# Regrouping the small matmuls of one hybrid encoder step: decode values in fours, state reads behind the scores, state updates over four banks

## The chip, the cores and the metric

The kernel runs on one core of one Trainium2 chip. The metric is the device time of one execution in microseconds (us), median of several. The kernel before took 2405.88 us (three runs, 2405.13 to 2412.4).

TensorE (PE) multiplies a stationary operand (at most 128 rows by 128 columns) with a moving one of up to 512 columns and writes into PSUM, which has eight banks of 512 fp32 values per partition. VectorE (DVE), ScalarE (ACT) and GpSimd (POOL) do the elementwise work. SyncE (SP), ACT and POOL issue DMA transfers; each of these queues works strictly in order, so a transfer that waits holds up whatever stands behind it.

## The reference

One step of a layer with two groups of eight heads, on a prompt of 1024 frames and on 8 running streams of 16 frames each (the "sample", 128 rows):

```python
h = rms_norm(x, norm_pre)
q_sb, k_sb, v_sb, gate_sb, q_r, k_r, v_r, gate_r = project(h, w_in, pos)   # 2048 x 8192
# stick-breaking heads; the sample has 1024 cached keys and values per stream
z = q @ k.T * d ** -0.5
a = where(strict, exp(log_sigmoid(z) + later(log_sigmoid(-z))), 0)
o_sb = a @ v
# retention heads, chunkwise; the sample starts from a state of 128 x 128 per stream and head
o_r   = (q_r k_r' * decay) @ v_r + decay_read * (q_r @ S)
S_new = gamma ** n * S + (k_r * decay_write)' @ v_r
y = concat(head_norm(o_sb) * silu(gate_sb), head_norm(o_r) * silu(gate_r)) @ w_out
x = x + rms_norm(y, norm_post)
```

For the sample this means, per head: scores against 8 x 1024 cached keys, a weighted sum over 8 x 1024 cached values, a read of eight 128 x 128 states, and an update of those eight states.

## The kernel before

**Groups and projections.** The rows are worked on in two groups: the first has four prompt tiles of 128 rows and the sample tile (640 rows), the second the other four prompt tiles. For every head of a group the kernel projects queries, keys, values and gates of both branches. Operands are split into a high and a low part, and each product is three matmuls (lines 227 and 286). These products fill PE; everything else is fitted between them. The accumulators `acc0` and `acc1` with two buffers each take four of the eight PSUM banks. The other four are two score banks (`psz`, tile `z`, used in turn by `score_tile`), one bank `psa` (tile `pa`, given by `acc_tile`) and one bank `psd` (tile `pd`, the decode sums).

**The hand-written clock.** Side work is written as Python generators, each wrapped in a `Job`. `tick()` is called once behind each of the product's three operand pairs at line 227, and once behind each group of three matmuls at line 286; it adds one to the clock and runs the first job that is due up to its next `yield`, whose number says after how many steps it wants to go on. A step is thus one pair of product matmuls in the first group. `drain(job)` calls `tick()` again and again without any product until a job has ended. It is called where the next head takes over a buffer: `ret_queries` drains the retention job behind its projection (line 910), `attention` drains the stick-breaking and the decode jobs (lines 934 and 949). Behind this stands the framework's own planner: it puts each engine's instructions in an order by what it takes to be ready, earlier program text first, so that an instruction may slip behind products that follow it in the text. `tied` and `issue_after` pin an instruction behind another one of its engine.

**The decode job** (lines 623 to 743), one per head, first group only. It loads the cached keys in 16 pieces of 128 x 512 from POOL's queue, transposes each on DVE, and after pieces 8 and 16 runs one score set at line 659: 16 instructions (8 fp32 matmuls, each two instructions) with 32 stationary columns, four streams side by side in the array's column strips. The pieces are `D_ZC` = 12 steps apart. Then come sigmoids, a product scan, a trip through DRAM that transposes the weights by blocks (`turn_out`, `turn_in`), and the value sum. The values are 8 tiles `vc` of 512 KB each, held in `V_BUFS` = 6 buffers and loaded by SP (line 687). The sum (lines 717 to 731) first multiplies the sample's own 128 rows (line 718) and then takes the 8 tiles two at a time: a pause of 18 steps, one set of 16 instructions with 32 stationary columns (line 726), and the loads of the next tiles into the buffers set free (tiles 6 and 7, behind the first set). Right behind the last set DVE copies the sum out of `pd` (lines 733 and 735).

**The retention job** (lines 745 to 857), one per head and group. For the sample it loads the states in four tiles `st` (two streams each), waits 18 steps, multiplies the sample's own part (line 810) and reads the states with 8 instructions of 32 columns (line 813), all into one `pa` bank. 9 steps later ACT and DVE take the result out, and the update follows in two halves, 9 steps apart: each takes the two score banks, multiplies with a contraction of 32 rows only (line 830, 8 instructions, two pairs of streams side by side in the array's row strips), lets DVE add to the states (line 833) and stores them. Then the output is normalised, turned through DRAM (32 + 32 steps) and gated; in doing so it writes the tiles `rk` and `rg`, which the next head uses again.

Of the kernel before, what the change touches and what calls it, by code (L numbers as in the profile page):

```python
# [9 lines left out]
F32 = mybir.dt.float32  # L10
F32R = mybir.dt.float32r
AF = mybir.ActivationFunctionType
ALU = mybir.AluOpType
# [3 lines left out]
P = 128  # L17
# [4 lines left out]
DS = 16  # L22
# [10 lines left out]
KC_AHEAD = 2  # L33
D_DEC = 2
D_NAT = (8, 11)
D_TR = (3, 7)
D_ZP = (2, 2)
D_Z0 = (19, 11)
D_AV = (9, 11)
# [2 lines left out]
D_KN = 40  # L42
D_VC = 9
V_BUFS = 6
D_RET = (9, 5)
D_TO = (32, 23)
D_TA = (14, 0)
# [7 lines left out]
LOG_GAMMA = [math.log(1.0 - 2.0 ** (-5.0 - h)) for h in range(H)]  # L55
# [3 lines left out]
def tile_hybrid_step(  # L59
# [26 lines left out]
    nc = tc.nc  # L86
# [61 lines left out]
    phase = [0]  # L148
# [151 lines left out]
    with ExitStack() as s1:  # L300
# [47 lines left out]
        with tc.tile_pool(name="p0", bufs=2) as p0, tc.tile_pool(name="p0s", bufs=1) as p0s, tc.tile_pool(  # L348
            name="p0p", bufs=4, space=PSUM
# [100 lines left out]
        psa = s1.enter_context(tc.tile_pool(name="psa", bufs=1, space=PSUM))  # L450
        psd = late.enter_context(tc.tile_pool(name="psd", bufs=1, space=PSUM))
# [108 lines left out]
        def stick_breaking(g, h, out, q2, k2, rest):  # L560
# [3 lines left out]
            for step in range(len(todo) + lag):  # L564
# [55 lines left out]
                    out.done(i)  # L620
                yield D_AV[phase[0]]

        def decode(h, qs, rest):
            i = 4
            out = Out(1, "do")
# [4 lines left out]
            n = PAST + P  # L630
# [21 lines left out]
            for m in range(-KC_AHEAD, 2 * NB + 1):  # L652
                if m > 0 and m % NB == 0:
                    s, _, _ = chunk(m - NB)
                    z = score_tile("zc")
                    for j in range(2):
                        for c in range(4):
                            r = slice(32 * c, 32 * c + 32)
                            mm = nc.tensor.matmul(  # L659
                                z[r, :],  # L660
                                qp[:, j, r],
                                ready[2 * j + c // 2][:, c % 2, :],
                                start=(j == 0),
                                stop=(j == 1),
                            )
                            if j == c == 0:

                                tc.add_manual_dep(
                                    mm.ins,
                                    turned.ins.name,  # L670
                                    mybir.DependencyInfo(
                                        mybir.DependencyClass.NoSync, mybir.DependencyReason.SCHED_ONLY
                                    ),
                                    reason="a set at a time",
                                )
                    ready = []
                    sigmoids(kp, be, s * 512, z)
                if 0 <= m < 2 * NB:
                    if m % 2 == 0:
                        ready.append(ip.tile([P, 2, 512], F32, name="kcT", tag="kv", bufs=V_BUFS))  # L680
                    turned = nc.vector.transpose(ready[-1][:, m % 2, :], loaded.pop(0))  # L681
                    yield D_ZC
                if m + KC_AHEAD < 2 * NB:
                    loaded.append(load(m + KC_AHEAD))
            def load_v(k):
                vc = ip.tile([P, NB, P], F32, name="vc", tag="kv", bufs=V_BUFS)
                ld = nc.sync.dma_start(
                    vc, cache_v[0, :, k * P : (k + 1) * P, h, :].rearrange("b p d -> p b d")
                )
                if 2 <= k < V_BUFS:  # L690
                    tied(ld)
                return vc
# [24 lines left out]
            po = psd.tile([P, 512], F32, name="pd", tag="pd")  # L717
            nc.tensor.matmul(po[:, 2 * P : 3 * P], at[:, 8, :], vn[:, i, :], start=True, stop=True)

            for k0 in range(0, 8, 2):  # L720
                yield 2 * D_VC
                for k in (k0, k0 + 1):
                    vc = values.pop(0)
                    for c in range(4):
                        r = slice(32 * c, 32 * c + 32)
                        nc.tensor.matmul(  # L726
                            po[r, : 2 * P], at[:, k, r], vc[:, 2 * c : 2 * c + 2, :], start=(k == 0), stop=(k == 7)
                        )
                for k in (k0, k0 + 1):
                    if k + V_BUFS < 8:  # L730
                        values.append(load_v(k + V_BUFS))
            od = out.o[:, 0, :]
            nc.vector.tensor_copy(od, po[:, 2 * P : 3 * P])
            for j in range(2):
# [65 lines left out]
        def sample_retention(h, out, sc, rq, rkn, rv):  # L800
            i = 4

            sts = []
            for c in range(4):
                st = ip.tile([P, 2, P], F32, name="st", tag="st", bufs=4)
                tied(nc.sync.dma_start(st, state_ret[0, 2 * c : 2 * c + 2, h].rearrange("b d e -> d b e")))
                sts.append(st)
            yield 2 * D_RET[phase[0]]
            po = acc_tile()
            nc.tensor.matmul(po[:, 2 * P : 3 * P], sc, rv[:, i, :], start=True, stop=True)  # L810
            for c in range(4):
                r = slice(32 * c, 32 * c + 32)
                nc.tensor.matmul(
                    po[r, : 2 * P], rq[:, i * P + 32 * c : i * P + 32 * c + 32], sts[c], start=True, stop=True
                )
            yield D_RET[phase[0]]
            od = out.o[:, i, :]
            nc.scalar.activation(od, po[:, 2 * P : 3 * P], AF.Copy)
            for j in range(2):
                nc.vector.scalar_tensor_tensor(  # L820
                    od, po[:, j * P : (j + 1) * P], dec[:, h, 2 + j : 3 + j], od, ALU.mult, ALU.add
                )
            out.done(i)

            for c0 in (0, 2):
                pS = [score_tile(f"pSs{c}", (P, 2, P)) for c in range(2)]
                for j in range(2):
                    for c in range(2):
                        r = slice(32 * (c0 + c), 32 * (c0 + c) + 32)
                        nc.tensor.matmul(pS[c][:, j, :], rkn[r, i + j, :], rv[r, i, :], start=True, stop=True)  # L830
                for c in range(2):
                    st, b = sts[c0 + c], 2 * (c0 + c)
                    nc.vector.scalar_tensor_tensor(
                        st, st, math.exp(LOG_GAMMA[h] * DS), pS[c], ALU.mult, ALU.add
                    )
                    nc.scalar.dma_start(s_sample[0, b : b + 2, h].rearrange("b d e -> d b e"), st)
                yield D_RET[phase[0]]

        def ret_branch(gi, g, h, rq, rk, rv, rest):
            nt = len(g["tiles"])  # L840
# [367 lines left out]
```

## Time and profile before

| | |
|---|---|
| median of three runs | 2405.88 us |
| span of the profiled execution | 2398.4 us |
| mean granted TensorE clock in it | 0.994 |
| PE busy | 2331.4 us, 97% |
| DVE, ACT, POOL busy | 52%, 38%, 27% |
| first group's heads (about 130 to 1235 us) | PE busy 1078.65 of 1105 us |

The profiled execution is 7.5 us shorter than the median of the runs. A row of the timeline reads: start, duration, engine, line, operation, output<-inputs, rows*columns of the stationary operand, the moving operand, count of instructions, and in brackets the idle time before it with what ended that. Durations of matmuls include their way through the array and overlap; what a matmul costs is read from one start to the next. A row of the waits reads: who waited for whom, us in total, times, longest.

### The profile page before, as it was taken

What the parts mean: (1) busy time and instruction counts of PE and PEld (TensorE: products, weight loads), DVE (VectorE), ACT (ScalarE), POOL (GpSimd) and SP (SyncE); (2) the same over time, 40 slices, a digit from 0 to 9 for tenths busy, and PEclk for the clock granted to TensorE, in tenths of its full rate; (3) what the DMA queues carried; (4) which work ended last, traced back from release to release, by engine and by line L of the source; (5) the groups of instructions that cost most, each with busy time, mean ns of one, the idle gap of its engine ahead of it and who ended that gap; (6) DMA issues with size and microseconds to landing.
All of it is one profiled execution on the core that took longest, in us unless ns stands there. A gap on an engine that the chain in (4) does not pass through costs nothing.

```text
span 2398.4 us, 40493 instructions
## 1 busy us (share of the span) xinstructions
PE 2331.4 (97%) x14832; PEld 2093.7 (87%) x14832; DVE 1257.5 (52%) x2434; ACT 919.6 (38%) x1933; POOL 643.0 (27%) x1029
## 2 busy tenths in 40 slices
PE   7999999999999999998999999999999999999998
PEld 7998899999999999988878889889898887878787
DVE  7245545445554555445545554554554665564544
ACT  6323333333333333324433434343343454543343
POOL 3144353444344353443202112020221230000000
PEclk9999999999999999999999999999999999999999
DMA  7658879797889879798975565565565666765554
GB/s 244 164 131 209 162 169 196 169 203 166 184 179 194 184 167 194 176 198 198 200 191 151 139 157 149 133 157 146 142 160 139 157 177 181 231 207 176 191 182 132
DMA packets 674890, 418.68 MB, mean 175 GB/s; under 512 B 224513, under 2 KB 619777, under 8 KB 672257
## 3 DMA queue, kind: packets, MB, share of 16 engines
q1 hardware_dynamic: 524272, 285.99, 47.8%
q0 software_dynamic: 32256, 71.36, 13.6%
q10 hardware_dynamic: 118160, 58.74, 9.1%
q8 instruction: 116, 1.90, 0.4%
q14 instruction: 86, 0.70, 0.1%
HBM read 336.24 MB, written 79.69 MB: 173 GB/s over the span
## 4 chain that ended last, share of the span: by engine, by line
PE 87%; DVE 4%; DMA 4%; issue 2%; ACT 1%; POOL 1%; ACTq 0%; DVEq 0%; SPq 0%; POOLq 0%
PE acc L227 45%; PE accn L286 17%; PE a L1029 5%; PE a L1030 5%; PE a L1028 5%; PE pa L616 3%; PE z L586 2%; DMA wr<-w_in 1%; PE zc L659 1%; PE pd L726 1%; DMA mr<-s_h 1%; DVE wl L130 1%; PE pa L770 1%; DVE out L1090 1%; PE rs L752 1%
## 5 line engine op out<-in xcount | busy, mean ns | idle before, releaser
L227 PE MATMUL acc<-mh,wh 128*128 128x256 f32 (+2 forms) x2304 | 664.3, 341 | 6.4 <-ACT wh L129 6.0
L227 PE MATMUL acc<-ml,wh 128*128 128x384 f32 (+2 forms) x2304 | 663.0, 340 | 0.0
L130 DVE TENSOR_TENSOR wl<-wr,wh 128x512 fp32r<-128x512 f32 (+1 forms) x576 | 392.7, 688 | 515.5 <-ACT wh L129 508.3
L227 PE MATMUL acc<-mh,wl 128*128 128x256 f32 (+2 forms) x2304 | 658.9, 339 | 0.6 <-DVE wl L130 0.5
L129 ACT ACTIVATE wh<-wr 128x512 fp32r<-128x512 f32 (+1 forms) x576 | 356.9, 624 | 713.1 <-PE acc L227 243.4
L227 PEld LDWEIGHTS acc<-mh,wh 128*128 128x128 f32 x2304 | 420.2, 189 | 43.3 <-ACT wh L129 7.1
L227 PEld LDWEIGHTS acc<-mh,wl 128*128 128x128 f32 x2304 | 424.4, 189 | 31.4 <-issue 2.1
L227 PEld LDWEIGHTS acc<-ml,wh 128*128 128x128 f32 x2304 | 422.6, 189 | 33.2 <-issue 5.3
L643 POOL DMA_DIRECT2D kc<-cache_sb_k x512 | 332.4, 655 | 369.8 <-DVE kcT L681 207.5
L286 PE MATMUL accn<-whn,mh 128*128 128x256 f32 x1152 | 329.0, 287 | 0.9 <-ACT whn L129 0.8
L286 PE MATMUL accn<-wln,mh 128*128 128x256 f32 x1152 | 326.2, 283 | 0.7 <-DVE wln L130 0.7
L286 PE MATMUL accn<-whn,ml 128*128 128x256 f32 x1152 | 326.0, 283 | 0.0
L286 PEld LDWEIGHTS accn<-whn,mh 128*128 128x128 f32 x1152 | 220.5, 192 | 10.8 <-issue 6.7
L1029 PE MATMUL a<-wl,mh 128*128 128x512 f32 (+1 forms) x576 | 219.7, 381 | 7.8 <-DVE wl L130 7.8
L286 PEld LDWEIGHTS accn<-wln,mh 128*128 128x128 f32 x1152 | 221.2, 192 | 1.7 <-DVE wln L130 0.9
L286 PEld LDWEIGHTS accn<-whn,ml 128*128 128x128 f32 x1152 | 221.2, 192 | 0.0
L1030 PE MATMUL a<-wh,ml 128*128 128x512 f32 (+1 forms) x576 | 218.9, 380 | 0.0
L1028 PE MATMUL a<-wh,mh 128*128 128x512 f32 (+1 forms) x576 | 218.0, 380 | 0.0
L130 DVE TENSOR_TENSOR wln<-wrn,whn 128x512 fp32r<-128x512 f32 x128 | 87.5, 687 | 119.2 <-ACT whn L129 118.5
L129 ACT ACTIVATE whn<-wrn 128x512 fp32r<-128x512 f32 x128 | 80.1, 633 | 152.2 <-PE accn L286 69.8
L1029 PEld LDWEIGHTS a<-wl,mh 128*128 128x128 f32 x576 | 108.3, 188 | 30.5 <-DVE wl L130 9.9
L479 POOL DMA_DIRECT2D be<-s_be x128 | 94.2, 742 | 132.7 <-DMA s_be<-be 114.7
(189 smaller groups left out, 2604.8 us busy)
## 6 DMA issues: line engine op xcount, KB each, us to landing
wr<-w_in SPq DMA_DIRECT2D x384, 256.0 KB, 4.2
wr<-w_out SPq DMA_DIRECT2D x184, 256.0 KB, 3.6
wrn<-w_in SPq DMA_DIRECT2D x128, 256.0 KB, 3.1
kc<-cache_sb_k POOLq DMA_DIRECT2D x512, 64.0 KB, 4.5
vc<-cache_sb_v SPq DMA_DIRECT2D x64, 512.0 KB, 8.6
xt<-x_prompt SPq DMA_DIRECT2D x8, 1024.0 KB, 5.6
xr<-x_prompt SPq DMA_DIRECT2D x8, 1024.0 KB, 6.2
out<-out ACTq DMA_DIRECT2D x12, 512.0 KB, 2.9
```

Source lines behind the costliest of these rows:

```text
L129: nc.scalar.activation(hi, src, AF.Copy)
L130: nc.vector.tensor_tensor(lo, src, hi.bitcast(F32), ALU.subtract)
L227: last = nc.tensor.matmul(a[:, :m], lhs[:, j, :], rhs[w][:, j, o : o + m], start=(w == 0 and j == 0 and n == 0), stop=(w == KT // WQ - 1 a ...
L286: anchor[0] = nc.tensor.matmul(a, lhs[q][:, jj, ts], rhs[:, j, :], start=(w == 0 and j == 0 and n == 0 and t % 2 == 0), stop=(w == KT // 2 ...
L479: q.dma_start(raw[32 * i : 32 * i + 32, :].rearrange("p (k a) -> p k a", a=32), s[:, :, 32 * i : 32 * i + 32].rearrange("k (j b) a -> b (k ...
L586: nc.tensor.matmul(z[:, :c], q2[a][:, i * P : (i + 1) * P], k2[b][:, s : s + c], start=(m == 0), stop=(m == 2),)
L616: nc.tensor.matmul(po[:, :P], at[:, j, :], vn[:, j, :], start=(j == 0), stop=(j == t))
L643: nc.gpsimd.dma_start(kc[32 * i : 32 * i + 32, :].rearrange("p (k d) -> p k d", d=32), cache_k[0, 2 * c + j, s * 512 : (s + 1) * 512, h, 3 ...
L659: mm = nc.tensor.matmul(z[r, :], qp[:, j, r], ready[2 * j + c // 2][:, c % 2, :], start=(j == 0), stop=(j == 1),)
L1028: nc.tensor.matmul(a[:, :width], hi[q][:, j, ts], wh, start=(k == 0), stop=False)
L1029: nc.tensor.matmul(a[:, :width], hi[q][:, j, ts], wl, start=False, stop=False)
L1030: nc.tensor.matmul(a[:, :width], lo[q][:, j, ts], wh, start=False, stop=(k == KT - 1))
```

## The change

Five things change, all in code that runs in the first group (the constants for the second group stay as they are):

- The value sum takes four key tiles at a time: two sets of 32 instructions, each after a pause of 36 steps, instead of four sets of 16 after 18. The loads of tiles 6 and 7 stand behind the first set of four.
- The copies out of `pd` come 6 steps after the last set (`D_SUM`), not at once.
- The state reads are put on a list. The decode job of whichever head is then running calls the list right behind the matmuls of its next score set, and pins the reads behind the last of them. The retention job looks every 2 steps whether that has happened, up to 70 times, and issues the reads itself if not. The sample's own part (line 810) moves behind the reads. The results are taken out 3 steps later (`D_OFF`) instead of 9.
- The state update is one set of 16 instructions over four banks (both score banks, `pa` and `pd`), with the first instruction of the older score bank in front and the rest pinned behind the first two; 3 steps later come DVE's four additions and the four stores.
- The pause in front of the transposed weights' use, `D_TR`, goes from 3 to 7 steps in the first group; it stands in the decode job in front of line 718 and in the stick-breaking job in front of its last value product.

```diff
-D_TR = (3, 7)
+D_TR = (7, 7)
...
+V_SET = 4
+D_SUM = 6
+N_READ = 70
+D_OFF = 3
...
+        waiting = []
+
+        def with_scores():
+            while waiting:
+                waiting.pop(0)()
...
                     ready = []
+                    with tc.issue_after(mm.ins):
+                        with_scores()
                     sigmoids(kp, be, s * 512, z)
...
-            for k0 in range(0, 8, 2):
-                yield 2 * D_VC
-                for k in (k0, k0 + 1):
+            for k0 in range(0, 8, V_SET):
+                yield V_SET * D_VC
+                for k in range(k0, k0 + V_SET):
                     vc = values.pop(0)
...
+            yield D_SUM
             od = out.o[:, 0, :]
...
             yield 2 * D_RET[phase[0]]
-            po = acc_tile()
-            nc.tensor.matmul(po[:, 2 * P : 3 * P], sc, rv[:, i, :], start=True, stop=True)
-            for c in range(4):
-                r = slice(32 * c, 32 * c + 32)
-                nc.tensor.matmul(
-                    po[r, : 2 * P], rq[:, i * P + 32 * c : i * P + 32 * c + 32], sts[c], start=True, stop=True
-                )
-            yield D_RET[phase[0]]
+            read = []
+
+            def read_states():
+                po = acc_tile()
+                for c in range(4):
+                    r = slice(32 * c, 32 * c + 32)
+                    nc.tensor.matmul(
+                        po[r, : 2 * P], rq[:, i * P + 32 * c : i * P + 32 * c + 32], sts[c], start=True, stop=True
+                    )
+                nc.tensor.matmul(po[:, 2 * P : 3 * P], sc, rv[:, i, :], start=True, stop=True)
+                read.append(po)
+
+            waiting.append(read_states)
+            for _ in range(N_READ):
+                if read:
+                    break
+                yield 2
+            if not read:
+                waiting.remove(read_states)
+                read_states()
+            po = read[0]
+            yield D_OFF
...
-            for c0 in (0, 2):
-                pS = [score_tile(f"pSs{c}", (P, 2, P)) for c in range(2)]
...
+            yield D_OFF
+            pS = [score_tile(f"pSs{c}", (P, 2, P)) for c in range(2)]
+            pS += [
+                pool.tile([P, 512], F32, name=f"p{n}", tag=f"p{n}")[:, : 2 * P].rearrange("p (j e) -> p j e", j=2)
+                for pool, n in ((psa, "a"), (psd, "d"))
+            ]
+            lead = None
+            for j in range(2):
+                for c in ((0, 1, 2, 3) if h % 2 else (1, 0, 2, 3)):
+                    r = slice(32 * c, 32 * c + 32)
+                    with tc.issue_after(lead.ins) if lead else nullcontext():
+                        mm = nc.tensor.matmul(pS[c][:, j, :], rkn[r, i + j, :], rv[r, i, :], start=True, stop=True)
+                    if j == 0 and c < 2:
+                        lead = mm
+            yield D_OFF
+            for c in range(4):
+                st, b = sts[c], 2 * c
+                nc.vector.scalar_tensor_tensor(st, st, math.exp(LOG_GAMMA[h] * DS), pS[c], ALU.mult, ALU.add)
+                nc.scalar.dma_start(s_sample[0, b : b + 2, h].rearrange("b d e -> d b e"), st)
+            yield D_RET[phase[0]]
```

More of the change, by code (lines that the diff above doesn't have):

```diff
@@ L728, in decode @@
                         )
-                for k in (k0, k0 + 1):
+                for k in range(k0, k0 + V_SET):
                     if k + V_BUFS < 8:
                         values.append(load_v(k + V_BUFS))
+            yield D_SUM
             od = out.o[:, 0, :]
@@ L823, in sample_retention @@
             out.done(i)
-            for c0 in (0, 2):
-                pS = [score_tile(f"pSs{c}", (P, 2, P)) for c in range(2)]
[L827 to L837, printed above, removed]
+            yield D_OFF
[18 more added lines that the diff above has]
+            yield D_RET[phase[0]]
         def ret_branch(gi, g, h, rq, rk, rv, rest):
```

## The prediction

> **What bounds the kernel now.** I read the page first, then the waits of PE in the first group, then the timeline of PE around each kind of small set, and last SP and DVE around the same places.
>
> ```profile
> PE 2331.4 (97%) x14832; PEld 2093.7 (87%) x14832; DVE 1257.5 (52%) x2434; ACT 919.6 (38%) x1933; POOL 643.0 (27%) x1029
> PE 87%; DVE 4%; DMA 4%; issue 2%; ACT 1%; POOL 1%; ACTq 0%; DVEq 0%; SPq 0%; POOLq 0%
> ```
>
> PE is busy for 97% of the span, and 87% of the chain that ended last is PE. Whatever shortens PE's own sequence shortens the run by as much, unless it opens a wait. The longest waits of PE between 130 and 1235 us (the first group's heads) are:
>
> ```profile
> PE pa L770 <- DVE sc L754: 5.5, 4, 4.2
> PE acc L227 <- ACT wh L129: 5.4, 1, 5.4
> PE pa L616 <- DVE kb L576: 4.0, 4, 3.3
> PE pa L813 <- DMA st<-state_ret: 2.8, 3, 2.3
> PE pSs L830 <- DVE st L833: 2.3, 1, 2.3
> ```
>
> They sum to 20 us of 1105, nearly all in single events at the first and the last head. In the six heads between, PE does not stand still, and the change must earn its time there from the number of switches between full-width products and narrow sets.
>
> **The change part by part.**
>
> *Values in fours.* Here are one of today's sets, a place where two sets ran back to back, and a second such place:
>
> ```profile
> 391.21 0.46 PE L227 MATMUL acc<-ml,wh 128*128 128x256 f32 x2
> 391.50 0.46 PE L227 MATMUL acc<-mh,wl 128*128 128x256 f32 x2
> 391.89 1.07 PE L726 MATMUL pd<-vc,kp 128*32 128x256 f32 x16
> 392.89 0.56 PE L227 MATMUL acc<-mh,wh 128*128 128x256 f32 x2
> 393.29 0.45 PE L227 MATMUL acc<-ml,wh 128*128 128x256 f32 x2
> ...
> 252.60 1.93 PE L726 MATMUL pd<-vc,kp 128*32 128x256 f32 x32
> ...
> 254.86 0.46 PE L227 MATMUL acc<-mh,wh 128*128 128x256 f32 x2
> ...
> 1202.58 1.93 PE L726 MATMUL pd<-vc,kp 128*32 128x256 f32 x32
> ```
>
> A pair of products takes 391.50 - 391.21 = 0.29 us. The set should start at 391.79 and starts at 391.89: 0.10 to get in. From its start to the second pair behind it are 393.29 - 391.89 = 1.40, of which 0.29 is one pair: 1.11, and 1.21 with the entry. For 32 instructions the same count is 254.86 - 252.60 - 0.29 = 1.97, and 2.07 with the entry. Two sets of 16 cost 2.42, one of 32 costs 2.07: a joint saves 0.35. The work inside (2.26 - 1.40 = 0.86 for 16 instructions) is the same; entry, exit and a slow first pair are what goes. The 512 instructions of line 726 are 32 sets; two pairs are joined already (the rows at 252.60 and 1202.58), so 30 runs become 16: 14 joints, 4.9 us. These rows show it directly, so I allow no spread.
>
> *State reads behind a score set.* Both are sets of 32 columns, so the reads should just go on. Now they stand alone:
>
> ```profile
> 261.35 0.38 PE L752 MATMUL rs<-rq,rk 128*128 128x128 f32 x2
> 261.49 0.54 PE L227 MATMUL acc<-mh,wh 128*128 128x256 f32 x2
> ...
> 302.58 0.38 PE L810 MATMUL pa<-rv,sc 128*128 128x128 f32 x2
> 302.90 0.64 PE L813 MATMUL pa<-st,rq 128*32 128x256 f32 x8
> 303.47 0.56 PE L227 MATMUL acc<-mh,wh 128*128 128x256 f32 x2
> 303.86 0.46 PE L227 MATMUL acc<-ml,wh 128*128 128x256 f32 x2
> ```
>
> From the reads' start to the second pair are 0.96, less a pair 0.67. Appended they cost half of the 0.86 above: 0.43. Sure is a saving of 0.24. The entry comes on top: line 810 to the set takes 0.32, where such an fp32 matmul gives way to a product after 0.14 (261.49 - 261.35), so 0.18 more: 0.42. The unknown is only whether line 810, now behind a narrow set, meets the slow start itself; but the score set's successor meets that today too. I take 0.40, eight times: 3.2 us (bounds 1.9 and 3.4).
>
> *One update set.* Today there are two of these per head:
>
> ```profile
> 305.92 0.46 PE L227 MATMUL acc<-mh,wl 128*128 128x256 f32 x2
> 306.31 0.71 PE L830 MATMUL pSs<-rv,rkn 32*128 32x128 f32 x8
> 306.95 0.56 PE L227 MATMUL acc<-mh,wh 128*128 128x256 f32 x2
> 307.36 0.46 PE L227 MATMUL acc<-ml,wh 128*128 128x256 f32 x2
> ```
>
> One costs 307.36 - 305.92 - 2 x 0.29 = 0.86. It contracts over 32 rows, and its two pairs of streams lie in two of the four row strips. With four banks all four strips are in hand. No row shows four row strips at work. If they run at once as the four column strips do (16 instructions in 0.86 us at line 726), the second set vanishes but for its issue: 0.80 saved. If only two run at once, the joint set must do the second half's work, about 0.71 - 0.27 = 0.44 (the set's duration less that of one instruction), and the saving is 0.42. I take 0.80, since the column strips are the nearest case: 8 x 0.80 = 6.4 us (bounds 3.4 and 6.9). The Trainium skill, TensorE: Matmul & The Clock Gate, section "Part 3: Packing small matmuls", speaks against the full amount: it gives 3.07 times, not 4, for four row tiles. By it the joint set would be a third longer inside, an estimate of 0.14 us, and the part would save 5.3 us.
>
> The switches sum to 4.9 + 3.2 + 6.4 = 14.5 us, bounds 10.2 and 15.2.
>
> *Waits that go.* Where the copies stand right behind the last value set, DVE waits for PE, and PE's next retention product waits for a DVE operation behind the copy:
>
> ```profile
> 540.63 0.29 DVE L733 COPY do<-pd 128x128 f32<-128x128 f32 x1 [5.08 <-PE pd L726]
> 541.77 0.49 PE L770 MATMUL pa<-rv,sc 128*128 128x128 f32 x2 [0.43 <-DVE sc L754]
> ```
>
> The 5.08 us cost DVE nothing; the 0.43 cost PE. The list has 5.5 us in four such waits, the longest 4.2, so three of about 0.43: 1.3 us, which six steps of delay (1.8 us) cover. I do not count on the 4.2.
>
> In the last head the reads meet a late state load:
>
> ```profile
> 1111.35 0.38 PE L810 MATMUL pa<-rv,sc 128*128 128x128 f32 x2
> 1114.06 0.90 PE L813 MATMUL pa<-st,rq 128*32 128x256 f32 x4 [2.33 <-DMA st<-state_ret]
> 1117.01 0.90 PE L227 MATMUL acc<-ml,wh 128*128 128x256 f32 x2
> 1130.08 1.92 PE L659 MATMUL zc<-kcT,qp 128*32 128x512 f32 x16 [0.53 <-DVE st L833]
> ```
>
> Line 810 to the next product takes 5.66 us, against 0.89 in the rows of head 1: 4.8 lost. Moved behind the score set at 1130 the reads find their states there. What is late next is the loading for the second group, which crowds this stretch (the score set waits 0.53 itself), so I count half: 2.4, bounds 0 and 4.8.
>
> *What is added.* The update set now needs four banks free at once, one of them the score bank that the score set has just filled. ACT's two sigmoids read it, and the 3 + 3 steps (1.8 us) in between are short. Four DVE additions in a row delay the weight splits behind them. `psa` and `psd` are held a little longer; the stick-breaking products wait for `psa`. I allow 2 us for all eight heads: one wait of the size of the two near 2.3 in the list; bounds 0, where products ahead in the order cover it, and 5, two such.
>
> Sum: -14.5 - 1.3 - 2.4 + 2 = about -16. The profiled 2398.4 becomes 2382; the runs' median lies 7.5 above the span, so 2405.9 - 16 = **2390**. Own range of this case: best -15.2 - 1.3 - 4.8 - 5.4 (the wait for `wh` at the group's end, which follows SP's wait for value buffers) = -27, 2379; worst -10.2 + 5 = -5, 2401.
>
> **The rivals.**
>
> *Half the gain.* Only two row strips work at once and the reads gain 0.24: 10.2 us of switches, and if the last head's wait only moves, 10.2 + 1.3 - 2 = 9.5 saved: **2396**. For it: no row shows four row strips. Against it: four column strips do run at once.
>
> *The values come too late.* Tiles 6 and 7 are loaded behind the first set and used in the last; the time between shrinks.
>
> ```profile
> 386.11 2.14 SPq L687 DMA_DIRECT2D vc<-cache_sb_v  x2
> 396.28 3.06 SPq L479 DMA_DIRECT2D so<-s_o  x4
> 399.38 0.90 SPq L747 DMA_DIRECT2D dT<-c_dt  x1
> ...
> DMA to landing us min/median/max: 6.0/8.6/12.4
> ```
>
> In the new order the second set starts 36 steps (10.5 us) plus the first set's 2.0 behind the first, and needs tile 7 another 1.3 later: 13.8 us. A load issued at once, 0.7 us behind the set's start as at 386.11, lands by 9.8 at the median and just in time at the maximum. But the first set, now four steps past 391.89, falls among other SP transfers. If those at 396.28 and 399.38 go first, tile 7 is issued near 400.8 and lands at 409.4, where PE needs it at 393.1 + 13.8 = 406.9: 2.5 us, in seven heads 17.5. Net -16 + 17.5: **2407**. Against it: the loads stand ahead of those transfers in the text wherever the first set comes first.
>
> *Slower: the held reads of the first head.* Its first score set has gone by when the reads are listed, so they wait for the second:
>
> ```profile
> 165.75 1.92 PE L659 MATMUL zc<-kcT,qp 128*32 128x512 f32 x16
> 213.45 0.42 DVE L323 TENSOR_TENSOR rq<-acc,cosT 128x256 f32<-128x256 f32 x1
> 217.09 1.92 PE L659 MATMUL zc<-kcT,qp 128*32 128x512 f32 x14
> 220.88 1.04 PE L659 MATMUL zc<-kcT,qp 128*32 128x512 f32 x2 [1.88 <-DVE kcT L681]
> 233.43 0.94 PE L616 MATMUL pa<-vn,kb 128*128 128x128 f32 x6 [3.34 <-DVE kb L576]
> ```
>
> The reads need the query tile `rq`, which head 1's rotation overwrites from 213 on. The text therefore drains the retention job there, some 50 steps without products, and the stick-breaking work of these steps comes ahead of the products. If PE takes it in that order, it idles from about 213 until the product of 233.43 can run: 20 us, less some 4 of work done in it, so 16 lost, as much as the change wins. The drain's last steps also come close to the value sum (second score set, then 18 + 32 + 32 + 7 steps), which today starts at 252.60; if that is drawn in, 39 us less 6 of work, 33 lost. From 16 on the change loses; the middle of the two, 25, gives 2405.9 - 16 + 25 = **2415**. Against it: the planner lets side work slip behind products, as the joined sets at 252.60 show, and head 1's `rq` banks are only needed again a whole projection (48 steps, 14 us) later.
>
> *It does not do what it says.* If the four banks come free apart and products slip between, the updates stay two sets and the reads go alone: only the values gain, 4.9: **2401**.
>
> **How the numbers follow.** About 0.3%, 7 us, is what can be told from no change here. My forecast gets 0.62 (0.60 faster, 0.02 same), half the gain 0.13 (0.11 faster, 0.02 same), late values 0.10 (0.06 same, 0.04 slower), held reads 0.11 (0.01 faster, 0.10 slower), not doing it 0.04 (same). That is faster 0.72, same 0.14, slower 0.14. The range 2378 to 2408 leaves out most of the held reads and small tails, 0.18.
>
> **What would show it.** Right: 16 runs of 32 at line 726; line 813 directly behind line 659 with about 0.43 us between its start and the end of its work; one run of 16 at line 830 that costs about 0.9, not 1.3; no wait of line 770 on `sc` near 540. Wrong: waits of line 726 for `vc`, of line 830 for a bank, or a PE gap of more than 10 us between 200 and 260. If the sets shrink as counted and the time does not follow, new waits have taken it.

## The result, and the profile after

The kernel after takes 2401.53 us (median of 22 runs, 2394.62 to 2407.73) beside 2404.91 for the kernel before, run beside it (22 runs): a ratio of 0.9982, 95% interval 0.9975 to 0.999. That is 3.4 us by the medians and 4.3 by the ratio, where 16 were forecast: the direction was right, but the gain lies inside what the prediction called no change (0.3%). The two profiled executions even stand the other way (span 2401.4 against 2398.4). Single executions of either kernel lie up to 7 us off their medians, and the span of the profiled one of before is 6.5 below its median, that of after 0.1, so the profiles are read here for single places, and the times for sums.

The page of the kernel after, busy times and the shares of the chain that ended last:

```profile
PE 2322.8 (97%) x14832; PEld 2095.8 (87%) x14832; DVE 1256.9 (52%) x2434; ACT 914.5 (38%) x1931; POOL 644.0 (27%) x1029
PE 77%; DMA 9%; DVE 5%; issue 4%; POOL 2%; ACT 2%; SPq 0%; DVEq 0%; ACTq 0%; POOLq 0%
```

PE does the same 14832 instructions in 8.6 us less (2331.4 before), yet its share of the chain falls from 87% to 77% and that of the DMAs grows from 4% to 9%. The sets got cheaper, and PE began to wait. The waits of PE between 130 and 1235 us (who waited for whom, us in total, times, longest), the five longest and some smaller ones that are used below:

```profile
PE pd L738 <- DMA vc<-cache_sb_v: 12.7, 4, 5.3
PE pa L620 <- DVE kb L580: 8.3, 6, 2.7
PE accn L290 <- DVE rg L317: 6.6, 1, 6.6
PE pd L730 <- DVE kp L724: 3.8, 2, 2.8
PE pa L620 <- DVE so L623: 2.7, 1, 2.7
PE pa L783 <- DVE sc L767: 1.0, 1, 1.0
PE pa L620 <- DVE st L868: 0.9, 1, 0.9
...
PE z L590 <- DVE st L868: 0.5, 1, 0.5
PE pSs L862 <- ACT kb L503: 0.4, 1, 0.4
```

The first five sum to 34.1, the five of before to 20.0; with all smaller rows the lists hold 37.8 and 25.3. So 12.5 us of new waits stand against the 14.5 us of switches that were counted. Not all of them need be the change's: the list of f1 below, which does the work of the kernel before, holds 30.3. Two large rows are new and matter below: the value set (now line 738) waits for its tiles, and the products of line 290 wait once, in the last head, for the gate `rg`.

**The switches did shrink as counted.** Timeline of PE after, one value set of four tiles:

```profile
539.02 0.46 PE L231 MATMUL acc<-ml,wh 128*128 128x256 f32 x2
539.41 1.93 PE L738 MATMUL pd<-vc,kp 128*32 128x256 f32 x32
541.27 0.56 PE L231 MATMUL acc<-mh,wl 128*128 128x256 f32 x2
541.68 0.45 PE L231 MATMUL acc<-mh,wh 128*128 128x256 f32 x2
```

By the prediction's count (from one pair of products to the second pair behind, less two pairs of 0.29) the set costs 541.68 - 539.02 - 0.59 = 2.07, the value forecast. Reads behind a score set, and the update set, in the same head:

```profile
447.76 1.93 PE L669 MATMUL zc<-kcT,qp 128*32 128x512 f32 x16
449.50 0.61 PE L828 MATMUL pa<-st,rq 128*32 128x256 f32 x8
450.05 0.49 PE L831 MATMUL pa<-rv,sc 128*128 128x128 f32 x2
...
452.76 0.28 PE L290 MATMUL accn<-whn,ml 128*128 128x256 f32 x1
452.97 0.38 PE L862 MATMUL pSs<-rv,rkn 32*128 32x128 f32 x2
...
453.85 0.28 PE L290 MATMUL accn<-wln,mh 128*128 128x256 f32 x1
```

The reads follow the score set without a gap, and 0.55 us after their start the next kind of matmul begins; a set's exit, which the score set pays with or without them, is in that (the 32 value instructions take 541.27 - 539.41 = 1.86, of which 2 x 0.86 = 1.72 is work: 0.14). That leaves 0.41 for the reads; 0.43 was forecast. The update set of 16 costs 453.85 - 452.76 - 2 x 0.12 (a product takes 0.12 here) = 0.85, as much as one half of 8 did before (0.86). Four row strips run in the time of two. The Trainium skill, TensorE: Matmul & The Clock Gate, section "Part 3: Packing small matmuls", has 3.07 times for four row tiles, by which, in the prediction's estimate, the set would have been some 0.14 longer; the trace does not show that.

**Where the gain was given back first.** The first head after:

```profile
252.23 2.80 PE L738 MATMUL pd<-vc,kp 128*32 128x256 f32 x48
260.31 1.08 PE L738 MATMUL pd<-vc,kp 128*32 128x256 f32 x8 [5.28 <-DMA vc<-cache_sb_v]
262.61 1.08 PE L738 MATMUL pd<-vc,kp 128*32 128x256 f32 x8 [1.22 <-DMA vc<-cache_sb_v]
264.00 0.41 PE L231 MATMUL acc<-ml,wh 128*128 128x256 f32 x1
264.22 0.42 PE L231 MATMUL acc<-mh,wl 128*128 128x256 f32 x1
```

48 instructions run without a product between: both sets of four, up to tile 5, back to back, though the text puts 36 steps between them. Then PE stands 5.28 and 1.22 us for tiles 6 and 7. SP's timeline shows when these were loaded:

```profile
252.93 1.01 SPq L699 DMA_DIRECT2D vc<-cache_sb_v  x2
```

They can be issued only when the first set has freed buffers, 0.7 us after its start, and there is no second pause left to cover the transfer. The steps between the sets had been used up without products: the reads of the first head wait for the second score set, so the retention job is still open when the next head wants its query tile, and `drain` counts the clock on for every job. Afterwards products are 0.21 apart instead of 0.147.

The granted clock says the same (columns: window, its length, busy us and instructions of PE, PEld, DVE, ACT, POOL, then the clock, DMA share, GB/s):

```profile
264.00:268.30 4.30, 4.30 (x22) 4.30 (x22) 3.35 (x11) 3.15 (x5) 2.52 (x4) 0.50 1.09 180
268.30:272.00 3.70, 3.70 (x23) 3.70 (x23) 3.25 (x10) 2.70 (x5) 2.59 (x4) 0.99 1.19 227
```

At half clock 22 products cost 22 x 0.067 = 1.5 us more, so the late tiles cost about 8 us here with the waits. The kernel before has a loss of its own in this head, 4.21 us for `sc` at 270.88 with 6.8 us at half clock around it, and that one is gone. What is left is read by counting products from one place to another: those that start between 228 and 288 us in the profile of before take 7.3 us longer after, and 2.2 longer in e5 below. The Trainium skill, the same page, section "Part 1: The HAM clock gate", says that an idle window of about 3.4 us halves PE's rate. The trace agrees for 5.28, but it also shows the clock halved behind shorter stalls, of 2.17 us (ending at 916.83) and of 1.83 us for tile 7 in head 6:

```profile
1080.10 0.64 PE L738 MATMUL pd<-vc,kp 128*32 128x256 f32 x8 [1.83 <-DMA vc<-cache_sb_v]
1080.75:1084.10 3.35, 3.35 (x13) 3.35 (x14) 1.71 (x5) 0.00 (x0) 3.13 (x5) 0.50 1.17 187
```

**Heads 1 to 6.** Counting the start of the same product in both traces, these heads take 4.0 us less than before (288 to 1076 us), where the switches in them count 11.4 (12 joints of 0.35, 6 reads of 0.40, 6 updates of 0.80). In this stretch the list of waits holds 1.9 us before and 7.2 after: mainly the stick-breaking value product (line 620) waiting for its weights, 0.7 before and 5.7 after. That the change makes these waits is not shown: the profile of the inert f1 (the slowest of its twelve executions) takes 7.3 us longer than that of before over the same products, and those of e5 and f2, which differ in one inert constant, 7.0 and 11.4 less. The timelines of head 2, before and then after (POOL, with the second score set of PE ahead of it):

```profile
485.84 1.92 PE L659 MATMUL zc<-kcT,qp 128*32 128x512 f32 x16
485.88 0.78 POOL L472 DMA_DIRECT2D s_be<-kb  x1 [0.51 <-DVE kb L516]
495.36 0.65 POOL L479 DMA_DIRECT2D kb<-s_be  x1
```

```profile
490.68 2.29 PE L669 MATMUL zc<-kcT,qp 128*32 128x512 f32 x16
494.34 0.29 POOL L508 TENSOR_SCALAR_AFFINE_SELECT kp<-kp 128x128 f32<-128x128 f32 x1 [9.07 <-ACT kp L502]
496.63 0.78 POOL L476 DMA_DIRECT2D s_be<-kb  x1
504.21 2.58 POOL L483 DMA_DIRECT2D kb<-s_be  x4 [4.86 <-DMA s_be<-kb]
```

The second score set comes 5 us later, POOL's queue takes the masking of the decode's weights ahead of the transfer that sends the stick-breaking weights out to be turned (496.63 against 485.88), and they come back some 9 us later (504.21 against 495.36). The edit never touched that code. Which part moves the set can be read from the number of products ahead of it in heads 2 to 6: it stands 30 or 44 products later after than before, 42 or 48 later in e1, within 11 of its old place in e2, e3 and e8, and e10 below, which takes only the sets of four out of e5, brings it back to within 15. So the sets of four move it. That this place costs time is not shown: e5 has it there too, and e10 is slower than e5.

**The last head.** The wait for the gate, on PE, and ACT's queue ahead of it:

```profile
1125.05 0.58 PE L290 MATMUL accn<-whn,mh 128*128 128x256 f32 x1 [6.63 <-DVE rg L317]
1121.48 0.63 ACT L133 ACTIVATE mh<-mr 128x512 fp32r<-128x512 f32 x1 [5.36 <-DMA mr<-s_h]
```

ACT stands 5.36 us for a load for the second group, works off three splits, and takes the gate at 1123.76 only; PE waits for the accumulators that the gate is read from. Every profiled kernel that holds the reads of the last head has this wait, of 1.4 to 7.3 us, and none of the others has it.

### The profile page after: what moved, and what is told of

Same layout as the page of the kernel before. It is cut to its first block, busy times and chain, and to the rows that moved or that the text cites. A ratio compares the mean times of both kernels' runs of the same rounds, so it can differ in the third digit from the quotient of the medians.

```text
span 2401.4 us, 40475 instructions
## 1 busy us (share of the span) xinstructions
PE 2322.8 (97%) x14832; PEld 2095.8 (87%) x14832; DVE 1256.9 (52%) x2434; ACT 914.5 (38%) x1931; POOL 644.0 (27%) x1029
## 4 chain that ended last, share of the span: by engine, by line
PE 77%; DMA 9%; DVE 5%; issue 4%; POOL 2%; ACT 2%; SPq 0%; DVEq 0%; ACTq 0%; POOLq 0%
PE acc L231 37%; PE accn L290 16%; PE a L1062 5%; PE a L1063 5%; PE a L1061 5%; DMA kb<-s_be 3%; PE pa L620 2%; PE z L590 2%; DMA wr<-w_in 1%; DMA s_be<-kb 1%; DMA mr<-s_h 1%; DMA vc<-cache_sb_v 1%; DMA ro<-s_o 1%; PE pd L738 1%; DVE wl L134 1%
## 5 line engine op out<-in xcount | busy, mean ns | idle before, releaser
L231 PE MATMUL acc<-mh,wh 128*128 128x384 f32 (+2 forms) x2304 | 668.8, 342 | 1.0 <-DVE rk L327 0.9
L231 PE MATMUL acc<-mh,wl 128*128 128x384 f32 (+2 forms) x2304 | 664.3, 340 | 0.0
```

Of the source, the lines that this page charges most:

```text
L231: last = nc.tensor.matmul(a[:, :m], lhs[:, j, :], rhs[w][:, j, o : o + m], start=(w == 0 and j == 0 and n == 0), stop=(w == KT // WQ - 1 a ...
```

## The experiments

All times are medians; ratios stand to the kernel before, run beside them.

| run | edit | us | ratio (95% interval) |
|---|---|---|---|
| e1_values | before, value sets of four and late copies | 2407.14 | 1.0001 (0.9986 to 1.0015) |
| e2_reads | before, reads behind a score set | 2420.35 | 1.0071 (1.0057 to 1.0084) |
| e3_update | before, one update set | 2399.14 | 0.9975 (0.9964 to 0.9986) |
| e4_two_six | after, value sets of 2 and 6 | 2423.33 | 1.008 (1.0067 to 1.0093) |
| e5_head0 | after, first head's reads not held | 2395.38 | 0.996 (0.9943 to 0.9977) |
| e7_dtr | after, `D_TR` back to 3 | 2401.53 | 0.9983 (0.997 to 0.9996) |
| e8_dtr_alone | before, `D_TR` 7 | 2402.31 | 0.9984 (0.9973 to 0.9994) |
| e9_copies | before, late copies | 2410.31 | 1.002 (1.0009 to 1.0031) |
| e10_twos | e5, value sets of two | 2406.04 | 1.0004 (0.9992 to 1.0017) |
| e11_last_twos | e5, sets of two in the last head | 2395.34 | 0.9968 (0.9956 to 0.9981) |
| e12_none_held | after, no reads held | 2400.55 | 0.9984 (0.9971 to 0.9996) |
| e13_copies_at_once | e5, copies at once | 2400.13 | 0.9974 (0.9963 to 0.9985) |
| f1_inert_before | before, `D_KN` 41 | 2405.08 | 1.0006 (0.9995 to 1.0017) |
| f2_inert_head0 | e5, `D_KN` 41 | 2395.66 | 0.9963 (0.9949 to 0.9976) |
| f3_keys_earlier | e5, `D_ZC` 11 | 2424.05 | 1.0084 (1.007 to 1.0098) |
| f4_head0_dtr | e5, `D_TR` 3 | 2394.01 | 0.9957 (0.9942 to 0.9972) |

**The parts, each alone on the kernel before.**

```diff
# e1_values
-            for k0 in range(0, 8, 2):
-                yield 2 * D_VC
+            for k0 in range(0, 8, V_SET):
+                yield V_SET * D_VC
...
+            yield D_SUM
# e2_reads
+                    with tc.issue_after(mm.ins):
+                        with_scores()
...
+            waiting.append(read_states)
# e3_update
-            for c0 in (0, 2):
+            pS += [
...
+                for pool, n in ((psa, "a"), (psd, "d"))
+            ]
```

> Value sets of four alone, copies 6 steps later; reads, updates and the pause D_TR as before. Theory (the switches gain what was counted, and tiles 6 and 7 come too late wherever the two sets run close together): twelve or so joints, -4.2 us and -1.3 us for the copies, against waits of line 726 for vc at the first and last head of 5 to 12 us with a slow clock behind them: +2 to +8 us in all, and the profile lists waits of the value sum for vc. Rival (the waits for vc come from the held reads of the first head, whose drain pushes the value sets together): no wait for vc over 1 us, -5 us.

> Reads behind a score set alone; updates in two halves and values in twos as before. Theory (reads are worth 0.4 us a head, the drain in the first head costs little in itself): -3 us for the switches, up to -4 us in the last head, no long wait between 200 and 260 us that the kernel before does not have: -3 to -7 us. Rival (the drain is what costs): +5 us or more, with the loss between 200 and 280 us.

> One update set over four banks alone, at its old place behind the reads. Theory: 0.80 us a head, -6.4 us, with the score products and the stick-breaking products waiting for banks under 0.5 us a head: -4 to -7 us. Rival (holding all four free banks is what makes the waits of the score and stick-breaking products, 1 us a head): 0 to +2 us, and these waits appear in heads 1 to 6.

The update alone gains 6.0 us by the ratio; 6.4 were counted. The values with the late copies gain nothing; as the copies alone cost 4.8 us (e9), e1 does not price the sets by themselves. Two of PE's waits in e1:

```profile
PE pa L775 <- DVE sc L759: 13.3, 7, 2.8
PE pd L730 <- DMA vc<-cache_sb_v: 5.9, 7, 1.7
```

Tiles are late in seven heads, by less than a microsecond in most and not at all in the first, and the retention product waits for `sc` in seven though the copies stand 6 steps later. The reads alone lose 17 us. Two of PE's waits in e2, and one of a head's update halves:

```profile
PE zc L669 <- DVE kcT L693: 7.6, 3, 2.8
PE pd L738 <- DMA vc<-cache_sb_v: 5.0, 2, 3.8
...
458.34 0.71 PE L856 MATMUL pSs<-rv,rkn 32*128 32x128 f32 x4
459.41 0.71 PE L856 MATMUL pSs<-rv,rkn 32*128 32x128 f32 x4
```

The tile waits of e2 (3.83 and 1.15 us) stand in the first head, where e1 has none, although e2 takes the values in twos: it is the held reads that make the tiles late there, whatever the size of the sets. By the count of products some 5 of the 17 us are lost between 228 and 288 us, so this part of the rival (the drain is what costs) holds, and 12 in heads 1 to 6, where the profile of the inert f1 also shows 7. What takes those is not shown: the second score set waits for its transposed keys in three heads, and the second half of this update is split and pays entry and exit twice; that the halves contend for the score banks is a guess. The parts do not add up: 0, +17, -6 and `D_TR`'s -4 (e8) would be +7, and together they make -4.

**The late tiles.** e4 loads tiles 6 and 7 early (a small first set), e5 takes the first head out of the held reads.

```diff
# e4_two_six
-            for k0 in range(0, 8, V_SET):
-                yield V_SET * D_VC
+            for k0, n in ((0, 2), (2, 6)):
+                yield n * D_VC
# e5_head0
-            for _ in range(N_READ):
+            for _ in range(N_READ if h else 0):
```

> The changed kernel with value sets of two and six tiles instead of four and four: as many sets, but tiles 6 and 7 are loaded behind the first two, 54 steps ahead of their set. Theory (late values): the waits for vc at the first head (6.5 us and the slow clock behind it), at 1078 (2.2 us) and at the last head (4.7 us and more) go, -8 to -15 us against the changed kernel, -12 to -18 us against the kernel before. Rival (another DMA is late next, weights above all, so that the gain is lost again): within 4 us of the changed kernel.

> The changed kernel, but the first head reads its states at once (N_READ counts as 0 there), so that head 1 need not drain the retention job. Theory (the held reads of the first head push both value sets together; the loss between 228 and 270 us is theirs): no two value sets in one run near 252 us, the wait for vc of 5.3 us near 260 gone, 6 to 10 us less than the changed kernel. Rival (any arrangement of this stretch costs as much: the kernel before also lost 8 us near 266): within 3 us of the changed kernel, with another long wait between 200 and 285 us.

e4's theory fell: 19 us slower than before. The tiles that it was to bring early are late in its first head as they were, and its longest wait is another:

```profile
PE pa L619 <- DVE kb L579: 17.0, 5, 5.7
...
PE pd L737 <- DMA vc<-cache_sb_v: 6.4, 2, 5.2
```

It moves the first value set by 18 steps, and with it what follows; which of this costs the time was not followed up. e5 stood in the main: the first head's waits for tiles are gone, and 0.22% (5 us) came back, a little under the 6 to 10 expected; the two intervals just touch, but f2 and f4 below, which hold the same edit, repeat it. Its rival had a point too: another wait, for `sc`, stands in this head again, as in the kernel before. Its first head (timeline of PE):

```profile
251.08 1.93 PE L738 MATMUL pd<-vc,kp 128*32 128x256 f32 x32
252.94 0.56 PE L231 MATMUL acc<-mh,wh 128*128 128x256 f32 x2
...
267.99 0.79 PE L783 MATMUL pa<-rv,sc 128*128 128x128 f32 x2 [3.66 <-DVE sc L767]
```

One set of four now stands alone, and products follow it at once. PE still waits 4.3 us for tiles in this run, nearly all of it once, in the last head.

**The small delays.**

```diff
# e7_dtr (on after), f4_head0_dtr (on e5); e8_dtr_alone is the reverse on before
-D_TR = (7, 7)
+D_TR = (3, 7)
# e9_copies (on before); e13_copies_at_once takes the line out of e5
+            yield D_SUM
```

> The changed kernel with the pause D_TR back at 3 steps. Theory (the late stick-breaking weights in heads 2 to 6 come from the order of POOL's transfers, not from this pause): the waits of line 620 on kb stay or grow to 9 us, 0 to +4 us against the changed kernel. Rival (the pause itself pushes the last value product into a busy stretch): these waits fall under 3 us, and 5 us are won.

> The kernel before with the pause D_TR of 7 steps and nothing else: no matmul set changes, so the counted gain is 0. Theory (the parts of the change cost what their own waits cost): -2 to +1 us, since the pause only moves products behind weights that come late. Rival (the planner sorts the queues anew on any edit, and each arrangement has its own waits): a shift of 5 us or more in either direction, with waits moved on lines that the edit does not touch.

> The kernel before with the copies of the decode sums 6 steps later and nothing else. Theory: the three waits of 0.43 us of the retention product on its scores go, 0 to -2 us. Rival (the planner sorts the queues anew on any edit): a shift of 5 us or more in either direction, on lines that the edit does not touch.

The longer `D_TR` is worth 4 us on the kernel before and nothing inside the change, with or without the held first head (e7 beside the kernel after, f4 beside e5). The late copies alone cost 5 us on the kernel before, and the wait that they were to remove stays: seven waits of the retention product for `sc`, 5.8 us.

**What the parts are worth in the best version.**

```diff
# e10_twos (on e5)
-V_SET = 4
+V_SET = 2
# e11_last_twos (on e5)
+            vs = V_SET if h < H - 1 else 2
# e12_none_held (on after)
-N_READ = 70
+N_READ = 0
```

> The changed kernel with the first head's reads at once, and the values in twos as before. Theory (the sets of four gain 4.9 us in switches and lose about 4 us by the late tiles 6 and 7 in the last head and 0.7 in head 6): equal to the kernel it is made from within 2 us, no wait for vc over 1 us, 30 sets or so at line 738. Rival (sets of four are a clear gain): 4 to 5 us slower. Rival (late tiles cost more than the joints gain): 3 us or more faster.

> The changed kernel with the first head's reads at once, and the values in twos in the last head alone, where both sets of four run back to back behind late weights and PE waits 4.0 us for tile 7. Theory: that wait goes, 2 to 5 us faster than the kernel it is made from. Rival (the loads of the second group's weights are late next on the same queue): within 1.5 us, with a wait of the products or of line 730 in its place between 1190 and 1235 us.

> The changed kernel with no reads held: each head reads its states at once, ahead of its sample's own part, and one update set follows. Theory (the reads gain 0.4 us a head by the joint and up to 4.8 us by the later state load in the last head): 3 to 8 us slower than the kernel with only the first head's reads at once, line 828 again as eight sets of its own. Rival (holding the reads pushes the second score set against its transposed keys, 0.6 us a head, so that it wins nothing): within 2 us.

> The changed kernel with the first head's reads at once and the copies of the decode sums right behind the last value set. Theory (the copies made the kernel before 5 us slower only by the order that they gave the queues): a shift of up to 5 us in either direction, without a clear sign; the waits of line 783 on sc come back at 0.4 us each. Rival (late copies cost time by themselves, through psd and the decode job's later end): 3 to 5 us faster.

In e5 the sets of four are worth 10.6 us by the ratios (e10 against e5), give or take 5 (an estimate from the two intervals), where the joints count 4.9, though e1 has them (with the late copies) at nothing. Holding the reads in heads 1 to 7 is worth 5.8 (e12 against e5, whose intervals overlap a little), and e12 ties with the kernel after: the held reads of the first head gave back all that the other seven won. Sets of two in the last head change nothing (e11), but they do not remove the wait either: PE stands 3.66 us for a tile until 1220.89 there, against 4.00 in e5, so what that wait costs stays open. The copies at once (e13) are 3.4 us slower than e5, but the intervals overlap: unsettled.

**Is it any edit, or the place of the side work?** Parts that don't add up could mean that every edit reshuffles the planner's order. `D_KN` 41 changes one constant off the path; `D_ZC` 11 brings the decode forward by one step at each piece of keys.

```diff
# f1_inert_before (on before), f2_inert_head0 (on e5)
-D_KN = 40
+D_KN = 41
# f3_keys_earlier (on e5)
-D_ZC = 12
+D_ZC = 11
```

> The kernel before with one step more before the keys are written out (D_KN 41 for 40): same work, same sets, nothing of the change. Theory (what the change gave back is the planner's new order, which any edit brings): a shift of 3 to 8 us in either direction, with other waits of PE on lines that the edit does not touch. Rival (the parts of the change themselves open the new waits): within 1.5 us.

> The changed kernel with the first head's reads at once, and the same idle edit (D_KN 41). Theory (planner's order): 3 to 8 us off the kernel it is made from, likelier slower since that one is the best so far. Rival (the parts set the time): within 2 us.

> The changed kernel with the first head's reads at once, and the cached keys 11 steps apart instead of 12, so that the second score set is asked for 8 steps earlier. Theory (its 0.6 us of wait for transposed keys in each of heads 2 to 7 comes from the order in which keys and the turned weights share POOL's queue, not from the spacing): the set runs at the same place with the same wait, within 3 us. Rival (spacing): the wait goes, 3 to 4 us faster.

> The changed kernel with the first head's reads at once, and the pause D_TR back at 3 steps. Theory (the pause is worth nothing by itself; 0 between the changed kernel and the same with 3 steps): within 3 us. Rival (with the first head's drain gone the pause decides when the value sets of four may start): 4 us or more slower or faster, with the waits of line 730 on kp changed.

The inert edit moves nothing that can be measured in the times of either kernel (f1's interval spans 1, f2 equals e5), so the theory that any edit does it fell. A small edit of the decode's own pauses does move the time: one step less per piece costs some 30 us against e5, where neither expectation had more than 4. The timeline of one head of f3, PE:

```profile
518.26 1.93 PE L738 MATMUL pd<-vc,kp 128*32 128x256 f32 x32
...
530.88 1.50 PE L738 MATMUL pd<-vc,kp 128*32 128x256 f32 x24
536.13 1.08 PE L738 MATMUL pd<-vc,kp 128*32 128x256 f32 x8 [3.75 <-DMA vc<-cache_sb_v]
537.85 0.74 PE L231 MATMUL acc<-mh,wl 128*128 128x256 f32 x2
538.38 0.73 PE L231 MATMUL acc<-mh,wh 128*128 128x256 f32 x2
```

And SP in the same head:

```profile
509.98 12.58 SPq L217 DMA_DIRECT2D wr<-w_in  x6
522.61 1.13 SPq L699 DMA_DIRECT2D vc<-cache_sb_v  x2
```

The first set runs at 518.26, but SP is inside six weight transfers until 522.56 and issues tiles 6 and 7 only then. The second set reaches for tile 7 at 532.4 and stands 3.75 us, and the products behind it go at half clock, 0.53 a pair. Five such waits sum to 14.3 us in f3, about half of its loss without the half clock behind them. This is the prediction's rival of late values, in the heads where it was expected, once the decode runs a little earlier.

## Why the prediction was right or wrong

- **Values, 4.9 us for 14 joints.** The price of a joint was right (2.07 for a set of 32). The sets of heads 1 to 5 run in one piece; those of the first head, of head 6 and of the last are broken by waits. What the sets of four bring depends on the rest: nothing in e1 together with the late copies, about 10.6 in e5.
- **Reads, 3.2 us.** Price right (0.41 against 0.43 appended). What failed is that the first head's reads cost more than this in another job.
- **Update, 6.4 us.** Right: 0.85 for the joint set, and -6.0 for that part alone. The four strips run at once, so the rival of half the gain fell in its reason, although the time came out nearer to it than to the forecast.
- **Copies, -1.3.** The waits for `sc` did shrink in the kernel after (5.5 to 1.0 us), but not by the mechanism named: in e9 the copies are late and the waits remain (5.8), as they do in e5 (6.5).
- **Last head's state load, -2.4.** That wait is gone from the list, as argued, but its time is not shown to be won: the waits of before there (2.33, 2.27 and 0.53) make room for the 6.63 for the gate and 0.44 for a bank. From 1090 to 1142 us the same products take 3.1 us less, but they take 2.1 less in the inert f1 as well. The stretch from 1141 to 1235 us is 4.1 us longer than in the profile of before. By the same count of products all kernels run here but f4 show such a difference (+4 to +16), the inert f1 too (+4.0), so the profile of before was a short one there, and the change is not charged with it.
- **What is added, 2 us, bounds 0 and 5. This is the step that failed.** It looked for the cost at the banks that the update set needs, and there PE waits for 1.8 us, as allowed (0.4 in front of the set; 0.9 and 0.5 where stick-breaking products wait for its additions). What it left out was what came of the side work's new places. The 14.5 + 1.3 + 2.4 = 18.2 us of the sum less the measured 4.3 make 14 us, seven times the allowance. Of these 14, some 5 are shown to be the tiles that the held reads make late in the first head: e5 gets them back. The terms for the copies and the state load, 3.7 together, are not seen to have come. The rest, some 5 against the 2 allowed, stays open: late weights in heads 1 to 6 and late tiles in head 6 and the last stand in the list, but no run takes them out alone, and single profiles differ by as much without any change.
- **Held reads, 2415.** The drain was foreseen, and that it would draw the value sum in; PE did not idle at 213, since products slipped ahead as argued. The price was 25 us. By e5 it is 5, and it is paid at the tiles, behind the drain; e2 shows the same tile waits with the values in twos.
- **It does not do what it says, 2401.** This is the time that came, by chance: the sets did join.
- **Late values, 2407.** The mechanism was right and its place wrong: not 2.5 us in seven heads, but 12.7 in three, of which 6.5 in the first. e1 and f3 show that the other heads are only some steps away from it. The prediction held these two rivals apart, but it was the first that brought about the second.

What stays open besides: why the planner puts the second score set later when the values come in fours, and whether that costs anything; where e2 loses its 17 us; and why a longer `D_TR` helps the kernel before. The best version is the change with the first head's reads issued at once: 0.996 (0.9943 to 0.9977) with `D_TR` 7 and 0.9957 (0.9942 to 0.9972) with 3, which cannot be told apart. Both beat the two kernels of the study, and still stand at some 10 us where 16 were counted.

## What to carry to other kernels

Price a merged set by its switches, but then ask what its larger bite delays: the loads that wait for the buffers it frees come later and are needed sooner, and a stall, here of 1.83 us or more, can be paid again at half clock. Where side work is timed by counted steps, look for whatever uses up steps without main work (a drain), since pauses that looked ample vanish there. Don't add up gains measured one part at a time, since here 0, +17, -6 and -4 made -4; take parts out of the whole instead.

## What the hardware showed that was not expected

Four row strips cost what two did (0.85 against 0.86 for twice the instructions). And the clock's answer to a stall is no fixed price. In f3 stalls of 3.75, 3.29 and 3.09 us halved the speed of the value instructions right behind them (8 of them in 1.08 us, not 0.64); behind one of 3.16 us these ran at full speed, and the half clock came 1.4 us after PE had resumed. In the kernel after a stall of 1.83 us was followed by 3.4 us at 0.50, and the clock stood at 0.50 until 8 us after PE had first resumed behind the stall of 5.28.
